# A hybrid decoder block: x handed over by feature as well and normed where it lands, weights handed over in blocks of 128 columns

## The chip, the cores and the metric

The kernel runs on one core of one Trainium2 chip. The metric is the device time of one execution in microseconds (us). A core has five engines that work beside one another: TensorE (PE: matmuls, with its weight loads PEld), VectorE (DVE), ScalarE (ACT), GpSimd (POOL) and SyncE (SP, which here only issues DMAs). Each engine takes its instructions in order. DMAs are issued from SP's and ACT's queues and move data between HBM and the on-chip memory SBUF; PE writes to PSUM, from where DVE and ACT read.

## What is computed

One decoder layer over x of 1024 tokens with 1024 features, float32. What the change touches is the beginning:

```python
def rms_norm(x, g):
    y = x * lax.rsqrt(jnp.mean(x * x, axis=-1, keepdims=True) + NORM_EPS)
    return y * g

u = rms_norm(h, mix_pre_g)                    # h is x here
z = jnp.einsum('bsd,de->bse', u, w_in)        # 1024 x 1024 by 1024 x 4096
p, q, k, v, gate_a, gate_b = (column ranges of z)
```

From q, k and v follows a differential attention of four heads, from p a pooling mixer; sigmoid gates merge both, an output projection, a residual with a norm, and a SwiGLU feed-forward with a hidden width of 2816 (w_ffn_gate, w_ffn_up, w_ffn_down) close the layer.

## The kernel before

Matmuls contract over the partitions, so u is needed by feature: 128 features on the partitions, tokens along the free dimension. Each float32 operand is split into a high part, rounded to the matmul's format (fp32r), and a low part, the rest; a product is three matmuls: high by high, high by low, low by high. `split` is an ACT copy (high) and a DVE subtract (low; `sub`, line 87).

The opening (lines 299 to 544) norms x and makes the first four of the 32 column blocks of z, which are q and k of heads 0 and 1 (f = 0 to 3), by plain matmuls. The rest of z is made by units (`unit`, `seven_steps`, line 271) that do two column blocks with seven block products in place of eight (Strassen's scheme). A unit needs the operands A11, A12, A21, A22 (the halves of u by token and by feature), their sums S1 to S4, and the like combinations B and T of two weight blocks; its products accumulate in PSUM banks X, Y and Z. Y takes its bank from the ring "mm", which the outputs of f = 2 and 3 also use; Z from "fil", which f = 0 and 1 use.

Inside the block `tc.manual_schedule` (line 463) the order of each of PE, ACT, DVE and POOL is the order in which the instructions are written. Outside it, and for SP, a planner with a cost model of its own sets the order. DMAs on ACT's queue stand in ACT's order.

In the opening, x comes in eight blocks of 128 tokens (tb = 0 to 7). For each: `stat` squares and sums it on ACT (`square`, line 363) and makes 1/rms (`rstd_of`, line 124: a DVE tensor_scalar, then a POOL pow); `normed` (line 371) multiplies the block by 1/rms, one number per partition, and by the gain g1, which was loaded onto all partitions, on DVE; `turn` (line 391) transposes it on PE in eight 128x128 steps into a PSUM pair; `take` (lines 405 to 421) copies it from there on ACT twice, as the high part of A and as a raw copy; `take_lo` makes the low part on DVE; `take_sums` (line 423), for the second half of the tokens, makes the sums on DVE. `feature(f, p)` is the product of block f with 256 tokens (p = 0 to 3): 24 matmuls (lines 357 for p = 0, 106 to 108 for the others). `store` (line 440) scales and splits its 512 columns (ACT and DVE), and `post` issues the store to `qkd` on ACT's queue. `first_raw`, `first_hi`, `first_lo` load and split the four weight blocks. `raw_weights` (line 211) loads 128 columns of a weight with 1024 rows: each of the 128 partitions gets eight runs of 512 bytes. `weights_steps` (line 216) makes the operands B and T of a unit. `constants` loads six small tensors on ACT's queue.

Of the kernel before, what the change touches and what calls it, by code (L numbers as in the profile page):

```python
# [39 lines left out]
def block_kernel(ctx, tc, x, w_in, pool_mix, pool_scale, w_branch_a, lam_q1, lam_k1, lam_q2,  # L40
# [4 lines left out]
    w_in, pool_mix, pool_scale, w_branch_a = w_in[0], pool_mix[0], pool_scale[0], w_branch_a[0]  # L45
# [3 lines left out]
        t[0] for t in (mix_pre_g, mix_post_g, ffn_pre_g, ffn_post_g))  # L49
    w_ffn_gate, w_ffn_up, w_ffn_down = w_ffn_gate[0], w_ffn_up[0], w_ffn_down[0]  # L50
# [262 lines left out]
    def w_cols(o, i):  # L313
        return w_in[:, o + i * P:o + (i + 1) * P]
# [6 lines left out]
    def qk_done(h, e, t, src, st=None, post=None):  # L321
        st = b4([P, 2, HALF], F32R, "qk_st") if st is None else st[e][:, :, half(t)]
        hi, lo = st[:, 0], st[:, 1]
        if e == 0:
            qs = 1.0 / (8.0 * 0.25 ** (h + 1))
            nc.scalar.mul(hi, src, qs)
            nc.vector.scalar_tensor_tensor(out=lo, in0=src, scalar=qs, in1=f32(hi), op0=ALU.mult, op1=ALU.subtract)
# [9 lines left out]
    plain, xts, xr = {}, [], []  # L337
# [14 lines left out]
    def common(h, e, t, o, c, by_pass):  # L352
        _, hi, lo = plain[h, e]
        if by_pass:
            for i, (w, a) in enumerate(((hi, 0), (hi, 1), (lo, 0))):
                for k in range(KD):
                    nc.tensor.matmul(o[:, c], w[:, k, :], U[f"A{t + 1}{k // 4 + 1}"][a][:, k % 4, c],
                                     start=i == 0 and k == 0, stop=i == 2 and k == KD - 1)
# [4 lines left out]
    def square(tb):
        ss = small(1, "ss")
        sumsq(xts[tb], ss)
        xr.append(ss)

    def rstd(tb):
        xr[tb] = rstd_of(xr[tb], 1, D)

    def normed(tb):
        nc.vector.scalar_tensor_tensor(out=xts[tb], in0=xts[tb], scalar=xr[tb], in1=g1, op0=ALU.mult, op1=ALU.mult)

    xts.append(load_x(0))
    xts.append(load_x(1))
    nc.sync.dma_start(g1, mix_pre_g.partition_broadcast(P))
    first_raw(0)
    xts.append(load_x(2))
    xts.append(load_x(3))
    first_raw(1)  # L380
    first_raw(2)
    xts.append(load_x(4))
    first_raw(3)

    turned = {}

    def stat(tb):
        square(tb)
        rstd(tb)

    def turn(tb):
        both = pair("x_t")
        for k in range(KD):
            nc.tensor.transpose(both[:, k // 4, k % 4 * P:(k % 4 + 1) * P], xts[tb][:, k * P:(k + 1) * P], ident)
        turned[tb] = [both[:, kq, :].rearrange("p (k t) -> p k t", k=4) for kq in range(2)]
        if tb + 5 < NB:
            xts.append(load_x(tb + 5))

    def token_cols(tb):
        return slice(tb % 4 * P, (tb % 4 + 1) * P)  # L400

    def raw_cols(tb, kq):
        return traws[(("A11", "A12"), ("S1", "S3"))[tb // 4][kq]][:, :, token_cols(tb)]

    def take_hi(tb):
        for kq in range(2):
            nc.scalar.copy(U[f"A{tb // 4 + 1}{kq + 1}"][0][:, :, token_cols(tb)], turned[tb][kq])
# [10 lines left out]
    def take_lo(tb):
        for kq in range(2):
            hi, lo = (a[:, :, token_cols(tb)] for a in U[f"A{tb // 4 + 1}{kq + 1}"])  # L420
            sub(lo, turned[tb][kq] if tb < 2 else raw_cols(tb, kq), hi)

    def take_sums(tb):
        s1, s2, s3, s4 = (traws[f"S{i + 1}"][:, :, token_cols(tb)] for i in range(4))
# [5 lines left out]
    outs, W = {}, {}  # L430
    wsteps = weights_steps(W, w_cols(o_q, 2), w_cols(o_k, 2))

    def feature(f, p):
        if p % 2 == 0:
            outs[f] = (fil if f < 2 else mm)("qk")
        common(*firsts[f], p // 2, outs[f], slice(p % 2 * 2 * P, (p % 2 + 1) * 2 * P), p == 0)

    posts = []

    def store(f, t):  # L440
        qk_done(*firsts[f], t, outs[f], post=posts)

    def post():
        posts.pop(0)()

    def sum_operand(*names):
        for n in names:
            U[n] = operand(n)
            split(U[n], traws[n])
# [12 lines left out]

    with tc.manual_schedule(engines={nc.tensor.engine, nc.scalar.engine, nc.vector.engine, nc.gpsimd.engine}):
        stat(0)
        stat(1)
        normed(0)
        turn(0)
        normed(1)
        turn(1)
        first_hi(0)  # L470
        take_hi(0)
        take_hi(1)
        first_lo(0)
        take_lo(0)
        take_lo(1)
        stat(2)
        normed(2)
        take_raw(0)
        feature(0, 0)
        first_hi(1)  # L480
        first_lo(1)
        take_raw(1)
        turn(2)
        stat(3)
        first_hi(2)
        normed(3)
        first_lo(2)
        feature(1, 0)
        take(2)
        stat(4)  # L490
        take_lo(2)
        turn(3)
        normed(4)
        first_hi(3)
        feature(2, 0)
        first_lo(3)
        take(3)
        stat(5)
        take_lo(3)
        turn(4)  # L500
        normed(5)
        take(4)
        stat(6)
        take_lo(4)
        take_sums(4)
        feature(3, 0)
        turn(5)
        take(5)
        normed(6)
        take_lo(5)  # L510
        stat(7)
        feature(0, 1)
        normed(7)
        take_sums(5)
        feature(1, 1)
        turn(6)
        store(0, 0)
        take(6)
        take_lo(6)
        take_sums(6)  # L520
        post()
        store(1, 0)
        next(wsteps)
        feature(2, 1)
        turn(7)
        take(7)
        constants()
        take_lo(7)
        post()
        store(2, 0)  # L530
        take_sums(7)
        feature(3, 1)
        post()
        store(3, 0)
        next(wsteps)
        post()
        sum_operand("S1")
        feature(0, 2)
        feature(1, 2)
        next(wsteps)  # L540
        feature(2, 2)
        sum_operand("S2")
# [8 lines left out]
        post()
        feature(1, 3)
        store(1, 1)
        sum_operand("S3")
        post()
# [93 lines left out]
    nc.scalar.mul(sgc, sgc, 1.0 - LAMBDA_INIT)  # L649
# [669 lines left out]
```

## Time and profile before

| what | us |
|---|---|
| median of 3 runs | 1265.39 (1264.96 to 1266.09) |
| the profiled execution | 1264.89 |
| its span, first to last instruction | 1263.0 |
| PE busy, DVE busy, ACT busy, POOL busy in the span | 1240.5, 822.2, 574.2, 226.6 |

The profile is one execution. Its page gives the busy time of each engine and the groups of instructions; the trace behind it can be asked for a timeline, for the waits of an engine (who it waited for; total, number, longest), and for windows of time. The granted clock of PE was 0.999 of the full one over the span. "128x512 f32" is a shape: partitions by elements.

### The profile page before, as it was taken

To read this page: it belongs to the slowest core of one execution; us is meant where nothing else is said; L and a number is where in the kernel's file an instruction comes from. 1 tells how busy PE (TensorE), PEld (TensorE's weight loads), DVE (VectorE), ACT (ScalarE), POOL (GpSimd) and SP (SyncE) were. 2 spreads that over 40 slices of the span, in tenths; PEclk is the share of its full clock that TensorE was granted. 3 is DMA by queue.
4 is the path that set the end of the run, shared out by engine and by line. 5 is a ranking of instruction groups with operands and counts; after the bars stand their busy time and mean duration, and the time that the engine had idled before them with its cause. 6 is when DMAs were issued, how large, how long until landed. Compare 5 with 4: busy or idle time off the path is not lost.

```text
span 1263.0 us, 15954 instructions
## 1 busy us (share of the span) xinstructions
PE 1240.5 (98%) x5952; PEld 1037.5 (82%) x5952; DVE 822.2 (65%) x1213; ACT 574.2 (45%) x1030; POOL 226.6 (18%) x237
## 2 busy tenths in 40 slices
PE   6999999999999999999999999999999999999997
PEld 6988778888888987888888888888888888888886
DVE  6895775445467776755697755656656537955666
ACT  7452344434567782444553333333333333554542
POOL 1000000000478861000102212112112011000221
PEclk9999999999999999999999999999999999999999
DMA  9263337234599213623315333233333368733235
GB/s 283 80 207 121 136 139 227 79 128 150 223 264 258 82 51 110 233 92 126 117 54 147 113 113 108 76 108 109 108 114 99 98 205 281 245 95 106 83 102 208
DMA packets 135566, 179.18 MB, mean 142 GB/s; under 512 B 7872, under 2 KB 90304, under 8 KB 133056
## 3 DMA queue, kind: packets, MB, share of 16 engines
q1 hardware_dynamic: 123552, 146.56, 37.2%
q10 hardware_dynamic: 11936, 31.60, 6.6%
q8 instruction: 47, 0.77, 0.3%
q14 instruction: 31, 0.25, 0.1%
HBM read 124.39 MB, written 53.74 MB: 141 GB/s over the span
## 4 chain that ended last, share of the span: by engine, by line
PE 87%; DVE 5%; ACT 3%; issue 2%; POOL 1%; DMA 0%; ACTq 0%; DVEq 0%; SPq 0%; POOLq 0%
PE Y L246 10%; PE Y L248 10%; PE Y L247 10%; PE X L246 5%; PE X L247 5%; PE X L248 5%; PE Yd L247 3%; PE Yd L248 3%; PE Yd L246 3%; PE o L812 3%; PE Z L248 2%; PE Z L247 2%; PE Z L246 2%; PE branch L248 2%; PE branch L247 2%
## 5 line engine op out<-in xcount | busy, mean ns | idle before, releaser
L164 DVE TENSOR_TENSOR p<-Z,p 128x512 f32<-128x512 f32 x35 | 24.2, 690 | 156.2 <-PE Z L248 154.5
L247 PE MATMUL Y<-A_lo,Wh 128*128 128x512 f32 x296 | 115.7, 391 | 0.3 <-DVE A_lo L87 0.3
L248 PE MATMUL Y<-A_hi,Wl 128*128 128x512 f32 x296 | 115.3, 389 | 0.1
L246 PE MATMUL Y<-A_hi,Wh 128*128 128x512 f32 x296 | 115.3, 390 | 0.0
L246 PE MATMUL Y<-S_hi,Wh 128*128 128x512 f32 x280 | 109.3, 390 | 0.0
L247 PE MATMUL Y<-S_lo,Wh 128*128 128x512 f32 x280 | 109.2, 390 | 0.0
L248 PE MATMUL Y<-S_hi,Wl 128*128 128x512 f32 x280 | 109.1, 389 | 0.0
L207 ACT CAST Wh<-wf_t 128x1024 fp32r<-128x1024 f32 x70 | 72.8, 1053 | 61.5 <-PE X L248 35.4
L87 DVE TENSOR_TENSOR Wl<-wf_t,Wh 128x1024 fp32r<-128x1024 f32 x70 | 86.9, 1247 | 13.9 <-PE Y L247 9.3
L87 DVE TENSOR_TENSOR w_op<-wd,w_op 128x512 fp32r<-128x512 f32 x77 | 56.3, 731 | 51.6 <-ACT w_op L168 51.4
L168 ACT CAST w_op<-wd 128x512 fp32r<-128x512 f32 x77 | 47.9, 622 | 71.4 <-PE Yd L248 31.2
L164 DVE TENSOR_TENSOR wf_t<-w_raw,wf_t 128x512 f32<-128x512 f32 x70 | 75.6, 1080 | 1.0
L247 PE MATMUL Yd<-w_op,s_op 128*128 128x512 f32 x176 | 68.7, 390 | 0.3 <-DVE w_op L87 0.2
L246 PE MATMUL Yd<-w_op,s_op 128*128 128x512 f32 x176 | 68.6, 390 | 0.0
L248 PE MATMUL Yd<-w_op,s_op 128*128 128x512 f32 x176 | 68.3, 389 | 0.0
L247 PEld LDWEIGHTS Y<-A_lo,Wh 128*128 128x128 f32 x296 | 55.6, 188 | 11.9 <-DVE A_lo L87 0.7
L248 PEld LDWEIGHTS Y<-A_hi,Wl 128*128 128x128 f32 x296 | 55.6, 188 | 11.9 <-DVE Wl L87 0.5
L246 PEld LDWEIGHTS Y<-A_hi,Wh 128*128 128x128 f32 x296 | 55.6, 188 | 11.6 <-ACT Wh L207 0.2
L168 ACT CAST s_op<-s_raw 128x512 fp32r<-128x512 f32 x77 | 47.5, 616 | 36.0 <-DMA s_raw<-fsd 23.3
L97 POOL TENSOR_TENSOR wb_lo<-wb_raw,wb_hi 128x1024 fp32r<-128x1024 f32 x4 | 10.5, 2632 | 291.8 <-DVE Wl L87 291.8
L246 PEld LDWEIGHTS Y<-S_hi,Wh 128*128 128x128 f32 x280 | 52.5, 188 | 12.1 <-ACT u L288 0.6
L248 PEld LDWEIGHTS Y<-S_hi,Wl 128*128 128x128 f32 x280 | 52.6, 188 | 10.9
(281 smaller groups left out, 3344.0 us busy)
## 6 DMA issues: line engine op xcount, KB each, us to landing
s_raw<-fsd SPq DMA_DIRECT2D x35, 512.0 KB, 3.8
w_raw<-in_w_in_dram SPq DMA_DIRECT2D x32, 512.0 KB, 4.2
w_raw<-in_w_ffn_gate_dram SPq DMA_DIRECT2D x22, 512.0 KB, 3.8
w_raw<-in_w_ffn_up_dram SPq DMA_DIRECT2D x22, 512.0 KB, 3.9
fsd<-fss SPq DMA_DIRECT2D x11, 1024.0 KB, 3.9
wd<-in_w_ffn_down_dram SPq DMA_DIRECT2D x44, 256.0 KB, 5.4
fsd<-F SPq DMA_DIRECT2D x33, 256.0 KB, 2.0
qkd<-qk_st ACTq DMA_DIRECT2D x16, 512.0 KB, 3.9
```

The costliest lines, as they stand in the source:

```text
L87: nc.vector.tensor_tensor(out=o, in0=a, in1=f32(hi), op=ALU.subtract)
L97: nc.gpsimd.tensor_tensor(out=lo, in0=raw, in1=f32(hi), op=ALU.subtract)
L164: nc.vector.tensor_tensor(out=o, in0=a, in1=b, op=op)
L168: nc.scalar.copy(hi, a)
L207: nc.scalar.copy(hi, a)
L246: nc.tensor.matmul(o, ah, bh, start=start, stop=False, skip_group_check=goes_on)
L247: nc.tensor.matmul(o, ah, bl, start=False, stop=False, skip_group_check=goes_on)
L248: nc.tensor.matmul(o, al, bh, start=False, stop=stop, skip_group_check=goes_on)
L812: nc.tensor.matmul(o, ats[b // 4][:, j, b % 4 * P:(b % 4 + 1) * P], V[:, b, :, :], start=b == 0 and j == 0, stop=b == qb and j == 1)
```

## The change

x is handed over a second time as `x_t`, by feature: four pieces of 256 tokens, each in two halves of 512 features (kq = 0, 1); on the chip a half is 128 partitions by 4 feature blocks by 256 tokens, and in memory each partition's 4 KB lie in one run. `w_in`, `w_ffn_gate` and `w_ffn_up` are handed over in blocks of 128 columns, in which the 4 KB of a partition also lie in one run. The gain comes as `g8`, 128 partitions by 8, one number for each feature.

x by token is still loaded and squared. 1/rms is now made for two token blocks at once (`rank`), copied along 128 columns on DVE, and turned by two PE transposes into a PSUM tile in which every partition holds 1/rms of the 256 tokens (`spread_rstd`). The piece is normed where it landed: for piece 0 one DVE instruction for each feature block multiplies by g8 and by the spread 1/rms (`normed_chunk`); for pieces 1 to 3 POOL multiplies by g8 (`scaled`, eight instructions a piece) and DVE by the spread 1/rms (`normed`, two a piece). High and low parts and sums are then made of 128x1024 each. The transposes of x and the raw copies are gone.

In the order: the four blocks' outputs are taken out of PSUM by two ACT instructions (`keep_raw`) and split later on DVE (`settle`), whose store to `qkd` goes to SP's queue; the loads of the constants go to SP too; the sums S1 to S4 are split in two halves each; the weights' steps of the first unit come later in the order; some arithmetic on constants that the planner placed moves to the end of the written order (`lambdas`).

```diff
     def raw_weights(src, tag):
         r = wp.tile([P, 2, 4, P], F32, tag=tag, bufs=2, name=name("w_raw"))
-        nc.sync.dma_start(r.rearrange("p h k n -> p (h k) n"), src.rearrange("(k p) n -> p k n", p=P))
+        nc.sync.dma_start(r.rearrange("p h k n -> p (h k n)"), src)
         return r
...
-    traws = {n: a8([P, 4, HALF], F32, n + "_raw") for n in ("A11", "A12", "S1", "S3")}
+    traws = {n: a8([P, 2, 4, 2 * P], F32, n + "_raw") for n in ("A11", "A12", "S1", "S3")}
     traws["S2"], traws["S4"] = traws["A11"], traws["A12"]
-    g1 = b4([P, D], F32, "g1")
+    g8 = cp.tile([P, KD], F32, name="g8")
+    nc.scalar.dma_start(g8, mix_pre_g)
...
     def w_cols(o, i):
-        return w_in[:, o + i * P:o + (i + 1) * P]
+        return w_in[o // P + i]
...
+    RAWS = (("A11", "A12"), ("S1", "S3"))
+    def raw_piece(p, kq):
+        return traws[RAWS[p // 2][kq]][:, p % 2]
+    def fetch_t(p, kq):
+        nc.sync.dma_start(raw_piece(p, kq).rearrange("p k t -> p (k t)"), x_t[p, kq])
...
+    def feature_pass(f, p, i):
+        _, hi, lo = plain[firsts[f]]
+        if p % 2 == 0 and i == 0:
+            outs[f] = (fil if f < 2 else mm)("qk")
+        w, a = ((hi, 0), (lo, 0), (hi, 1))[i]
         for k in range(KD):
-            nc.tensor.transpose(both[:, k // 4, k % 4 * P:(k % 4 + 1) * P], xts[tb][:, k * P:(k + 1) * P], ident)
...
+            nc.tensor.matmul(outs[f][:, piece_cols(p)], w[:, k, :], operand_piece(p, k // 4)[a][:, k % 4, :],
+                             start=i == 0 and k == 0, stop=i == 2 and k == KD - 1)
+    def feature(f, p):
+        for i in range(3):
+            feature_pass(f, p, i)
...
+    def square(p):
+        ss = small(2, "ss")
+        for i in range(2):
+            sumsq(xts.pop(2 * p + i), ss[:, i:i + 1])
+        ranks[p] = ss
+    def rank(p):
+        ranks[p] = rstd_of(ranks[p], 2, D)
+    def spread_rstd(p):
+        r = ranks[p]
+        rep = sm.tile([P, 2, P], F32, tag="sg", bufs=2, name=name("rep"))
+        nc.vector.tensor_copy(rep, r.unsqueeze(2).to_broadcast([P, 2, P]))
+        o = pair("r")[:, 0, :2 * P]
+        for i in range(2):
+            nc.tensor.transpose(o[:, i * P:(i + 1) * P], rep[:, i, :], ident)
+        spread[p] = o
+    def normed_chunk(p, k):
+        v = raw_piece(p, k // 4)[:, k % 4, :]
+        nc.vector.scalar_tensor_tensor(out=v, in0=v, scalar=g8[:, k:k + 1], in1=spread[p], op0=ALU.mult, op1=ALU.mult)
+    def scaled(p, kq):
+        for k in range(4):
+            v = raw_piece(p, kq)[:, k, :]
+            nc.gpsimd.tensor_scalar(v, v, g8[:, 4 * kq + k:4 * kq + k + 1], None, op0=ALU.mult)
+    def normed(p):
         for kq in range(2):
-            nc.scalar.copy(U[f"A{tb // 4 + 1}{kq + 1}"][0][:, :, token_cols(tb)], turned[tb][kq])
...
+            v = raw_piece(p, kq)
+            tt(v, v, spread[p].unsqueeze(1).to_broadcast([P, 4, 2 * P]), ALU.mult)
+    def piece_hi(p, kq):
+        nc.scalar.copy(operand_piece(p, kq)[0], raw_piece(p, kq))
+    def piece_lo(p, kq):
+        hi, lo = operand_piece(p, kq)
+        sub(lo, raw_piece(p, kq), hi)
+    def chunks(kq):
+        for k in range(4):
+            normed_chunk(0, 4 * kq + k)
+        piece_hi(0, kq)
...
+    def keep_raw(f, t):
+        h, e = firsts[f]
+        st = kept[f, t] = b4([P, 2, HALF], F32R, "qk_st")
+        qs = 1.0 / (8.0 * 0.25 ** (h + 1)) if e == 0 else 1.0
+        nc.scalar.mul(st[:, 0], outs[f], qs)
+        nc.scalar.mul(f32(st[:, 1]), outs[f], qs)
+    def settle(f, t):
+        h, e = firsts[f]
+        st = kept.pop((f, t))
+        sub(st[:, 1], f32(st[:, 1]), st[:, 0])
+        nc.sync.dma_start(qkd[h][e][:, :, half(t)], f32(st))
...
     def constants():
-        nc.scalar.dma_start(psc, pool_scale.rearrange("(g p) -> p g", p=P))
...
+        nc.sync.dma_start(psc, pool_scale.rearrange("(g p) -> p g", p=P))
```

SP's loads are written in the order x 0, x 1, x_t (0,0), weight 0, x_t (0,1), weights 1 and 2, x 2, x 3, weight 3, x_t (1,0), (1,1), x 4, x 5, x_t (2,0), (2,1), x 6, x 7, x_t (3,0), (3,1). The written order of the four other engines now reads (calls side by side, in order):

```python
square(0); rank(0); spread_rstd(0); first_hi(0); chunks(0); chunks(1)
feature_pass(0, 0, 0); first_lo(0); first_hi(1); piece_lo(0, 0); piece_lo(0, 1)
feature_pass(1, 0, 0); feature_pass(0, 0, 1); first_hi(2); first_lo(1); feature_pass(0, 0, 2); square(1)
feature_pass(1, 0, 1); first_lo(2); rank(1); scaled(1, 0); scaled(1, 1)
feature_pass(1, 0, 2); first_hi(3); first_lo(3); feature_pass(2, 0, 0); feature_pass(2, 0, 1)
spread_rstd(1); feature_pass(2, 0, 2); normed(1); piece_hi(1, 0); piece_hi(1, 1); square(2)
feature(3, 0); piece_lo(1, 0); piece_lo(1, 1); scaled(2, 0); rank(2); scaled(2, 1)
feature(0, 1); feature_pass(1, 1, 0); spread_rstd(2); feature_pass(1, 1, 1); feature_pass(1, 1, 2)
normed(2); square(3); piece_hi(2, 0); piece_hi(2, 1); scaled(3, 0); rank(3); scaled(3, 1)
piece_lo(2, 0); piece_lo(2, 1); keep_raw(0, 0); keep_raw(1, 0); feature(2, 1); feature_pass(3, 1, 0)
spread_rstd(3); normed(3); feature_pass(3, 1, 1); feature_pass(3, 1, 2); keep_raw(2, 0)
piece_hi(3, 0); piece_hi(3, 1); piece_lo(3, 0); piece_lo(3, 1); settle(0, 0); settle(1, 0)
feature(0, 2); keep_raw(3, 0); piece_sums(0); feature(1, 2); next(wsteps); settle(2, 0); settle(3, 0)
piece_sums(1); sum_operand("S1"); feature(2, 2); next(wsteps); feature(3, 2); sum_operand("S2"); next(wsteps)
feature(0, 3); keep_raw(0, 1); feature(1, 3); keep_raw(1, 1); sum_operand("S3"); constants(); next(wsteps)
feature(2, 3); keep_raw(2, 1); feature(3, 3); keep_raw(3, 1); next(wsteps, None); sum_operand("S4"); lambdas()
```

After it, outside the written order, come the four last calls of settle.

More of the change, by code (lines that the diff above doesn't have):

```diff
@@ L363, in square @@
[L363 to L392, printed above, removed]
-        for k in range(KD):
[L394 to L400, printed above, removed]
@@ L418, in take_lo, with piece_cols, operand_piece @@
[L418 to L424, printed above, removed]
+    def piece_cols(p):
+        return slice(p % 2 * 2 * P, (p % 2 + 1) * 2 * P)
+    def operand_piece(p, kq):
+        return [a[:, :, piece_cols(p)] for a in U[f"A{p // 2 + 1}{kq + 1}"]]
@@ new lines, in block_kernel @@
+    ranks, spread = {}, {}
+    def square(p):
[13 more added lines that the diff above has]
+        spread[p] = o
@@ L428, in take_sums @@
         tt(s4, s4, s2, ALU.subtract)
[L430 to L449, printed above, removed]
@@ L463, in block_kernel @@
[L463 to L542, printed above, removed]
@@ new lines, in sum_operand @@
+    def sum_operand(n):
+        U[n] = operand(n)
+        for j in range(2):
+            split([t[:, :, j * 2 * P:(j + 1) * 2 * P] for t in U[n]], traws[n][:, j])
+    kept = {}
+    def keep_raw(f, t):
[9 more added lines that the diff above has]
+        nc.sync.dma_start(qkd[h][e][:, :, half(t)], f32(st))
@@ new lines, in block_kernel @@
+    fetch_x(0)
+    fetch_x(1)
+    fetch_t(0, 0)
+    first_raw(0)
+    fetch_t(0, 1)
+    first_raw(1)
+    first_raw(2)
+    fetch_x(2)
+    fetch_x(3)
+    first_raw(3)
+    fetch_t(1, 0)
+    fetch_t(1, 1)
+    fetch_x(4)
+    fetch_x(5)
+    fetch_t(2, 0)
+    fetch_t(2, 1)
+    fetch_x(6)
+    fetch_x(7)
+    fetch_t(3, 0)
+    fetch_t(3, 1)
+    wsteps = weights_steps(W, w_cols(o_q, 2), w_cols(o_k, 2))
+    with tc.manual_schedule(engines={nc.tensor.engine, nc.scalar.engine, nc.vector.engine, nc.gpsimd.engine}):
+        square(0)
+        rank(0)
+        spread_rstd(0)
+        first_hi(0)
+        chunks(0)
+        chunks(1)
+        feature_pass(0, 0, 0)
+        first_lo(0)
+        first_hi(1)
+        piece_lo(0, 0)
+        piece_lo(0, 1)
+        feature_pass(1, 0, 0)
+        feature_pass(0, 0, 1)
+        first_hi(2)
+        first_lo(1)
+        feature_pass(0, 0, 2)
+        square(1)
+        feature_pass(1, 0, 1)
+        first_lo(2)
+        rank(1)
+        scaled(1, 0)
+        scaled(1, 1)
+        feature_pass(1, 0, 2)
+        first_hi(3)
+        first_lo(3)
+        feature_pass(2, 0, 0)
+        feature_pass(2, 0, 1)
+        spread_rstd(1)
+        feature_pass(2, 0, 2)
+        normed(1)
+        piece_hi(1, 0)
+        piece_hi(1, 1)
+        square(2)
+        feature(3, 0)
+        piece_lo(1, 0)
+        piece_lo(1, 1)
+        scaled(2, 0)
+        rank(2)
+        scaled(2, 1)
+        feature(0, 1)
+        feature_pass(1, 1, 0)
+        spread_rstd(2)
+        feature_pass(1, 1, 1)
+        feature_pass(1, 1, 2)
+        normed(2)
+        square(3)
+        piece_hi(2, 0)
+        piece_hi(2, 1)
+        scaled(3, 0)
+        rank(3)
+        scaled(3, 1)
+        piece_lo(2, 0)
+        piece_lo(2, 1)
+        keep_raw(0, 0)
+        keep_raw(1, 0)
+        feature(2, 1)
+        feature_pass(3, 1, 0)
+        spread_rstd(3)
+        normed(3)
+        feature_pass(3, 1, 1)
+        feature_pass(3, 1, 2)
+        keep_raw(2, 0)
+        piece_hi(3, 0)
+        piece_hi(3, 1)
+        piece_lo(3, 0)
+        piece_lo(3, 1)
+        settle(0, 0)
+        settle(1, 0)
+        feature(0, 2)
+        keep_raw(3, 0)
+        piece_sums(0)
+        feature(1, 2)
+        next(wsteps)
+        settle(2, 0)
+        settle(3, 0)
+        piece_sums(1)
+        sum_operand("S1")
+        feature(2, 2)
+        next(wsteps)
@@ L547, in block_kernel @@
         feature(3, 2)
+        sum_operand("S2")
+        next(wsteps)
         feature(0, 3)
-        store(0, 1)
-        next(wsteps)
[L551 to L555, printed above, removed]
+        keep_raw(0, 1)
+        feature(1, 3)
+        keep_raw(1, 1)
+        sum_operand("S3")
+        constants()
+        next(wsteps)
         feature(2, 3)
-        store(2, 1)
+        keep_raw(2, 1)
+        feature(3, 3)
+        keep_raw(3, 1)
         next(wsteps, None)
-        post()
@@ L560, in block_kernel @@
-        feature(3, 3)
-        store(3, 1)
         sum_operand("S4")
-        post()
+        lambdas()
+    for f in range(4):
+        settle(f, 1)
     later = []
```

79 lines of the change are left out of this document (35 added, 44 removed).

## The prediction, made before the change was timed

> **What bounds the kernel now.** The page comes first: its span line, the busy time of each engine and the row of PE in 40 slices.
>
> ```profile
> span 1263.0 us, 15954 instructions
> PE 1240.5 (98%) x5952; PEld 1037.5 (82%) x5952; DVE 822.2 (65%) x1213; ACT 574.2 (45%) x1030; POOL 226.6 (18%) x237
> PE   6999999999999999999999999999999999999997
> ```
>
> TensorE (PE) is busy in every slice but the first and the last. The PE waits come next: the first three rows are of the window 0 to 67.83 us, the others of the rest.
>
> ```profile
> PE x_t L394 <- DVE xt L372: 9.6, 3, 8.8
> PE qk L106 <- DVE qk_st L327: 1.1, 1, 1.1
> PE qk L357 <- ACT A_hi L407: 0.7, 1, 0.7
> ...
> PE oT L846 <- DVE O L833: 1.1, 2, 0.8
> PE y L106 <- ACT yh L168: 1.0, 2, 0.7
> PE h_t L1114 <- DVE og L1108: 0.7, 1, 0.7
> ```
>
> No row after the opening names a DMA, and these sum to a few microseconds. So the later weight loads are covered by PE work, and their new layout is worth nothing to the end; what the change does must come from the opening. That is what the timeline of PE shows, up to the first product of the first Strassen unit (X at 67.83):
>
> ```profile
> 8.75 3.53 PE L394 MATMUL x_t<-ident,xt 128*128 128x128 f32 x16 [8.75 <-DVE xt L372]
> 12.96 1.22 PE L357 MATMUL qk<-A_hi,w_hi 128*128 128x256 f32 x8 [0.68 <-ACT A_hi L407]
> 14.18 1.34 PE L357 MATMUL qk<-A_lo,w_hi 128*128 128x256 f32 x8
> ...
> 16.87 1.07 PE L394 MATMUL x_t<-ident,xt 128*128 128x128 f32 x8 [0.41 <-DVE xt L372]
> 17.69 1.20 PE L357 MATMUL qk<-A_hi,w_hi 128*128 128x256 f32 x8
> 18.73 1.12 PE L357 MATMUL qk<-A_lo,w_hi 128*128 128x256 f32 x8
> 19.69 1.12 PE L357 MATMUL qk<-A_hi,w_lo 128*128 128x256 f32 x8
> 67.83 0.40 PE L246 MATMUL X<-S_hi,Wh 128*128 128x512 f32 x1
> ```
>
> ```profile
> core 0: us, PE busy (x) PEld busy (x) DVE busy (x) ACT busy (x) POOL busy (x), PEclk, DMA share, GB/s
> 0.00:12.96 12.96, 3.53 (x17) 3.28 (x17) 5.01 (x9) 6.31 (x10) 1.80 (x8) 1.00 0.84 277
> 12.96:67.83 54.87, 52.81 (x433) 51.61 (x433) 47.98 (x75) 35.62 (x59) 4.82 (x10) 1.00 0.50 158
> 67.83:86.88 19.05, 19.05 (x85) 15.29 (x84) 16.02 (x19) 12.11 (x16) 0.00 (x0) 1.00 0.59 180
> ```
>
> The opening is 12.96 us before the first product and 54.87 us of products. A pass of 8 takes 0.96 us (18.73 to 19.69), 0.12 each, so the 384 take 46.1. The six later turns take about 0.82 each (16.87 to 17.69), 4.9 together. The remaining 3.9 us are slow first passes (12.96 to 14.18 is 1.22) and waits. VectorE (DVE) is busy for 48 of these 55 us, so it is the next bound. From 67.83 on PE is full, and what X gains the end gains.
>
> **The start.** x(0) and x(1) still come first, so the two squares stay where they are. Rows of ACT, DVE and POOL, then two windows of DMA rate:
>
> ```profile
> 4.58 1.06 ACT L132 ACTIVATE junk<-xt 128x1024 bf16<-128x1024 f32 x1 [2.58 <-DMA xt<-in_x_dram]
> 5.93 1.06 ACT L132 ACTIVATE junk<-xt 128x1024 bf16<-128x1024 f32 x1 [0.20 <-DMA xt<-in_x_dram]
> 7.11 0.15 DVE L127 TENSOR_SCALAR ms<-ss 128x1 f32<-128x1 f32 x1 [1.19 <-ACT junk L132]
> 7.34 0.56 POOL L128 TENSOR_TENSOR rstd<-ms,mhalf 128x1 f32<-128x1 f32 x1 [0.78 <-DVE ms L127]
> ```
>
> ```profile
> 3.00:5.00 2.00, 0.00 (x0) 0.00 (x0) 0.00 (x0) 0.42 (x1) 0.00 (x0) 1.00 1.04 420
> 12.00:15.00 3.00, 2.33 (x17) 1.81 (x16) 2.60 (x6) 2.68 (x6) 0.14 (x1) 1.00 1.17 299
> ```
>
> Rows of x alone came at 420 GB/s (3 to 5 us), loads mixed with weights at 299. In the changed kernel x, x by feature and weights all lie in 4 KB runs, so I take 1.27 us for each 512 KB (524 KB / 420 = 1.25); the other end is 1.75 (524 / 299). From 4.5 us on: x(1) 5.8, the two first feature pieces 7.0 and 9.6, weights 8.3, 10.9, 12.1 and 15.9, x(2) 13.4, x(3) 14.7, second feature pieces 17.2 and 18.5, last one 28.6. The 32-byte rows of g8 on ACT's queue land beside these.
>
> Durations for the new operations, and two pairs in which DVE and GpSimd (POOL) meet:
>
> ```profile
> L87 DVE TENSOR_TENSOR ml<-m,mh 128x256 fp32r<-128x256 f32 x32 | 12.5, 420 | 23.9 <-ACT mh L962 23.9
> L372 DVE SCALAR_TENSOR_TENSOR xt<-xt,rstd,g 128x1024 f32<-128x1024 f32 x8 | 10.2, 1282 | 2.2 <-POOL rstd L128 2.1
> L87 DVE TENSOR_TENSOR w_lo<-w_raw,w_hi 128x1024 fp32r<-128x1024 f32 x4 | 4.9, 1221 | 0.9 <-ACT w_hi L346 0.9
> L164 DVE TENSOR_TENSOR S_raw<-S_raw,S_raw 128x512 f32<-128x512 f32 x4 | 2.7, 683 | 0.0
> L781 POOL TENSOR_SCALAR E<-E,rec,cf 128x256 f32<-128x256 f32 x4 | 2.2, 558 | 0.4
> L829 POOL TENSOR_TENSOR rstd<-ms,mhalf 128x4 f32<-128x4 f32 x2 | 2.0, 1019 | 5.9 <-DVE ms L828 5.8
> ```
>
> ```profile
> 383.27 2.13 POOL L782 TENSOR_TENSOR E<-E,E 128x896 f32<-128x896 f32 x1
> 383.76 1.66 DVE L827 SCALAR_TENSOR_TENSOR ms<-esum 128x8 f32<-128x8 f32 x1
> ```
>
> ```profile
> 22.41 1.29 DVE L87 TENSOR_TENSOR A_lo<-A_raw,A_hi 128x512 fp32r<-128x512 f32 x2
> 22.57 0.93 POOL L128 TENSOR_TENSOR rstd<-ms,mhalf 128x1 f32<-128x1 f32 x1 [3.38 <-DVE ms L127]
> ```
>
> After the squares (7.1): one tensor_scalar and a pow over two columns, which lies between 0.56 (128x1) and 1.02 (128x4); I take 0.65, so 8.2. The spreading copy of 128x256 is not in the trace: at least the 0.15 of a one-column row, at most the 0.42 of a 128x256 subtract; 0.35. Two cold transposes at 0.22 (16 in 3.53) give 9.5. Each chunk of 128x256 costs 0.42, with 0.34 from start to start (the rows of DVE overlap by about 0.08); four end at 11.0, eight at 12.3. ScalarE's (ACT) cast of 128x1024 (at most the 1.06 of a square of that shape) ends at 12.1. **The first product starts at 12.2**, against 12.96, and the second half of its pass waits until 13.6 for the other cast. So the start itself gains 0.8 at most.
>
> **PE after that.** 384 products, 46.1. Six transposes remain, three spreads of 0.22: 0.7. The cold passes: before lost 0.26 in the first (1.22 against 0.96); here no run of 16 transposes stands ahead, so I take 1.2 over the first three, with 0 and 2.4 as ends. Waits, found by laying each engine's instructions in the written order at these durations: 0.6 for the other half of the first piece, 0.2 for w_hi(1), 0.1 for piece 1's second cast, 1.1 and 0.3 at spreads 2 and 3, whose copy stands behind rank on POOL. Sum: 12.2 + 46.1 + 0.7 + 1.2 + 2.3 = **62.5 us for the end of the products**, against 67.83.
>
> What is late next is piece 1: its columns land at 18.5, POOL scales eight chunks (at 0.60 with issue, 4.8 for a piece), DVE multiplies twice 1.2 and ACT casts; all is there at 26.6, and PE wants it at 26.5. Pieces 2 and 3 are wanted 11.5 us apart (96 products at 0.12), and none of the engines needs more than 6 for one, so they are hidden.
>
> **DVE.** After 12.3 it has, up to the low part of T1 and T3 that X needs: 12 subtracts of 128x1024 for weights and pieces at 1.14 (1.22 long, 1.14 apart) 13.7, six multiplies at 1.2 7.2, three copies 1.1, ranks 0.2, four settles at 0.6 2.4, eight sums of 128x1024 at 1.14 9.1, S1 and S2 4.6, two weight subtracts 2.3 and two differences 1.2: 41.8, so 54.1 without a wait. Waits add 8.0 (2.1 before the spread of piece 1, 3.1 around that of piece 2, the rest shorter). That is 62.1. **X can start at 62.6**, behind the products, and DVE has 0.4 us to spare, where before the same subtract ended 8.6 us ahead of X:
>
> ```profile
> 58.03 1.22 DVE L87 TENSOR_TENSOR Wl<-wf_t,Wh 128x1024 fp32r<-128x1024 f32 x1
> ```
>
> **Edits at nothing.** ACT loses 16 copies of 128x512 and gains eight for keep_raw; it waits for DVE, not the other way. The six constant loads and the eight stores go past ACT to SP, where behind them stand only weight loads for a unit that starts 19 us later; on ACT they held the queue ahead of the 1.1 us wait for qk_st, and that goes. The constants' arithmetic stands at the end of DVE's order; the four last settles (2.4) follow, with unit 2's weights behind them, needed near 82. Without that slack the 2.4 would count. Against the profiled run, X moves from 67.83 to 62.6: 5.2 us. That run took 1264.89 (span 1263.0 and 1.9 around it), and the median shown is 0.5 above it. **Forecast: 1259.7 us.**
>
> **The lock.** DVE's 8-column operation took 1.66 and ended with POOL's (385.42 against 385.40), and POOL's pow took 0.93 instead of 0.56 beside a subtract. One waits for the other. I have counted this where the 24 scalings meet a subtract or the copy: 0.9 us in the 62.5, which would be 61.6 if they never waited. The multiplies by spread are counted as free of it; if they too held POOL off, pieces 1 and 2 would each come 1.2 later (one multiply beside the scalings of each), and X would start near 64. The Trainium skill (SBUF — State Buffer, "SBUF: two separate sides") has it that the port pair these two engines share is locked for a whole instruction, by a GpSimd operation or by a DVE one with two SBUF inputs. By that rule a multiply whose second operand lies in PSUM takes no lock, so the sum would stay at 62.5, and every subtract that meets a scaling is paid in full; both quoted pairs agree with it, and no row of this trace has a multiply of this form beside POOL.
>
> **Rivals.**
> 1. **Slower: the scalings on POOL become the bound.** For: nothing in the opening put elementwise work on POOL, and the 0.93 row shows a wait of 0.37 on a 0.56 operation. At 0.93 for each, piece 1 is ready 2.6 us later (8 x 0.33), piece 3's spread, behind 16 more, costs 2.7, and X, which must then wait for T1 and T3, starts near 69.3 to 70, 1.5 to 2.2 after before's 67.83: 1266.4 to 1267.1, and each further 0.1 adds 2. It decides from about 0.78 on each; below that the kernel still gains. Against: the 558 ns row holds in the attention, where DVE works beside POOL, and the scaling there has two scalars and two operations against one here. Chance 0.12.
> 2. **The first unit takes Y first.** Y's bank is freed by keep_raw(2,1), which on ACT stands behind the cast of T2 and T4, and that behind DVE: 65.3. PE then waits 2.8 us: 1262.5, with a late DVE 1264. Against: before starts with X and Z, which use other banks. Chance 0.12.
> 3. **The pieces come at the mixed rate.** At 1.6 to 1.75 us for 512 KB, products end at 64.6 to 66.3: 1261.8 to 1263.5. For: 299 GB/s at 12 to 15 us. Against: those loads had rows of 512 bytes. Chance 0.12.
> 4. **More is gained.** Scalings at 0.5, no cold passes, Z ahead of X: 61 to 60: 1257.5. Chance 0.14.
> That x is not transposed any more is certain from the code; the forecast itself has 0.50.
>
> **How the numbers follow.** The forecast's own range is 1258.5 to 1261.5. For 8 in 10 I leave out the slower end of the first rival and half of the best case: 1257.3 to 1265. A measurement of this kernel can tell 0.2%, 2.5 us. Faster by more than that is below 1262.9: forecast 0.50, the best case 0.14, half of the second rival and of the third, 0.12: 0.76, taken down to 0.70 for waits I have not seen, which go to the two other cases. Slower (above 1267.9): half of the first rival, 0.06, and 0.03 of those waits. The rest, 0.21, is no change.
>
> **What would show it.** The x_t transposes are gone; eight transposes write r; the first qk product starts at 12.2 and X (or Z) near 62.6; POOL shows 24 tensor_scalar of 128x256 near 0.56; the PE waits in the opening stay under 0.7 each but at spread 2. Wrong: scalings at 0.8 or more, a PE wait over 2 us for A_hi of the second piece or for Wl at X, or a first Y that waits for qk_st.

## The result, and the profile after

| what | before | after |
|---|---|---|
| median, us (12 runs each) | 1265.32 (1264.81 to 1266.09) | 1268.48 (1267.74 to 1270.18) |
| the profiled execution, us | 1264.89 | 1268.47 |
| its span, us | 1263.0 | 1266.7 |

The ratio is 1.0026 (95% interval 1.0018 to 1.0034): the change makes the kernel slower by 3.2 us. The forecast was 1259.7 with a range up to 1265.0. The first two lines are of the page after, the third is the POOL row of before:

```profile
PE 1237.8 (98%) x5896; PEld 1034.7 (82%) x5896; DVE 821.3 (65%) x1207; ACT 571.2 (45%) x1018; POOL 250.1 (20%) x257
POOL 4400000000468861000102212112112011000221
POOL 1000000000478861000102212112112011000221
```

PE has 56 instructions less than before (64 transposes out, 8 in) and POOL 20 more (24 scalings in, four pows out); the first two slices of the row are the opening. Where the time went shows in windows cut at two marks: the first X product and the first Yd product (the last of the three large parts, w_ffn_down). First before, then after; the columns are those of the window rows in the prediction.

```profile
0.00:67.83 67.83, 56.35 (x449) 54.89 (x449) 52.99 (x83) 41.92 (x68) 6.62 (x18) 1.00 0.57 181
67.83:1045.59 977.76, 973.82 (x4583) 809.66 (x4581) 619.07 (x898) 434.39 (x776) 192.62 (x196) 1.00 0.42 136
1045.59:1263.00 217.41, 210.30 (x925) 173.00 (x923) 150.12 (x233) 97.91 (x188) 27.34 (x23) 1.00 0.49 158
```

```profile
0.00:69.68 69.68, 53.14 (x393) 52.06 (x393) 45.78 (x56) 34.54 (x48) 29.94 (x38) 0.95 0.56 214
69.68:1048.27 978.59, 974.12 (x4583) 809.67 (x4582) 625.31 (x919) 438.70 (x784) 192.75 (x196) 1.00 0.41 136
1048.27:1266.70 218.43, 210.57 (x925) 173.00 (x923) 150.22 (x233) 97.94 (x188) 27.36 (x23) 0.99 0.50 158
```

Of the 3.7 us by which the spans differ, 1.85 lie ahead of X, 0.83 in the long middle and 1.02 in the tail. In the opening PE is busy 3.2 us less than before, as meant, and still X starts later, not 5.2 us earlier. The waits of PE up to X, after:

```profile
PE r L398 <- DVE rep L395: 10.9, 2, 8.3
PE qk L374 <- ACT A_hi L416: 5.6, 3, 2.8
```

8.3 and 2.8 are the start, before the first product. The others are 2.61 for the fourth spread, 2.42 for the second piece and 0.35. What the first two of these wait for is on POOL, whose timeline after has no gap from 18.11 to 46.6 us:

```profile
18.11 0.71 POOL L128 TENSOR_TENSOR rstd<-ms,mhalf 128x2 f32<-128x2 f32 x1 [10.17 <-DVE ms L127]
18.81 8.12 POOL L408 TENSOR_SCALAR A_raw<-A_raw,g 128x256 f32<-128x256 f32 x8
26.92 5.22 POOL L408 TENSOR_SCALAR S_raw<-S_raw,g 128x256 f32<-128x256 f32 x4
32.11 0.73 POOL L128 TENSOR_TENSOR rstd<-ms,mhalf 128x2 f32<-128x2 f32 x1
32.83 9.01 POOL L408 TENSOR_SCALAR S_raw<-S_raw,g 128x256 f32<-128x256 f32 x8
41.80 0.72 POOL L128 TENSOR_TENSOR rstd<-ms,mhalf 128x2 f32<-128x2 f32 x1
42.53 3.75 POOL L408 TENSOR_SCALAR S_raw<-S_raw,g 128x256 f32<-128x256 f32 x4
46.24 0.41 POOL L473 IOTA cnt<- 128x16 f32 x4
```

The 24 scalings fill 26.1 us, 1.09 each, where the forecast had 0.60. DVE, whose multiplies need them, runs without a gap from the last of these multiplies up to X:

```profile
26.97 1.22 DVE L164 TENSOR_TENSOR A_raw<-A_raw,r 128x1024 f32<-128x1024 f32 x1 [2.39 <-POOL A_raw L408]
46.31 1.22 DVE L164 TENSOR_TENSOR S_raw<-S_raw,r 128x1024 f32<-128x1024 f32 x1 [1.64 <-POOL S_raw L408]
68.67 1.22 DVE L87 TENSOR_TENSOR Wl<-wf_t,Wh 128x1024 fp32r<-128x1024 f32 x1
```

The chain is this: the last scaling ends at 46.28, the last multiply starts at 46.31, and 22 us of DVE work behind it end at 69.89 with the low part that X needs. PE comes to X with its own products at the same time and does not wait; the second of these rows is the first product that reads the low part:

```profile
69.68 0.40 PE L246 MATMUL X<-S_hi,Wh 128*128 128x512 f32 x1
70.14 0.39 PE L248 MATMUL X<-S_hi,Wl 128*128 128x512 f32 x1
```

POOL waits for nothing after 18.11 and DVE for nothing after 46.31, so by this profile a faster PE would have brought that product forward by 0.25 us at most.

### The profile page after: what moved, and what is told of

Same layout as the page of the kernel before. It is cut to its first block, busy times and chain, and to the rows that moved or that the text cites. A ratio compares the mean times of both kernels' runs of the same rounds, so it can differ in the third digit from the quotient of the medians.

```text
span 1266.7 us, 15858 instructions
## 1 busy us (share of the span) xinstructions
PE 1237.8 (98%) x5896; PEld 1034.7 (82%) x5896; DVE 821.3 (65%) x1207; ACT 571.2 (45%) x1018; POOL 250.1 (20%) x257
## 4 chain that ended last, share of the span: by engine, by line
PE 47%; DVE 1%; issue 1%; POOL 1%; DMA 0%; ACT 0%; DVEq 0%; POOLq 0%; ACTq 0%
PE Y L247 6%; PE Y L248 6%; PE Y L246 6%; PE X L246 3%; PE X L247 3%; PE X L248 3%; PE Yd L247 3%; PE Yd L248 3%; PE Yd L246 3%; PE Z L247 2%; PE Z L248 2%; PE Z L246 2%; PE Xd L248 2%; PE Xd L246 2%; PE Xd L247 2%
## 5 line engine op out<-in xcount | busy, mean ns | idle before, releaser
L87 DVE TENSOR_TENSOR Wl<-wf_t,Wh 128x1024 fp32r<-128x1024 f32 x70 | 86.8, 1248 | 15.3 <-PE Y L247 9.8
```

The costliest lines, as they stand in the source:

```text
L87: nc.vector.tensor_tensor(out=o, in0=a, in1=f32(hi), op=ALU.subtract)
```

## The experiments

All times are medians in us. The kernel before was timed beside them on the same chip: 1265.26 beside the first four, then 1265.41 (the unread input, the filled waits, the early ranks), 1265.44 (the two kernels after that) and 1265.27 (the tail's edit alone, in both kernels).

**What a scaling costs.** Three kernels ask for it. The first gives the scaling a second scalar from memory (a column of ones) and a second multiply:

```diff
-            nc.gpsimd.tensor_scalar(v, v, g8[:, ...], None, op0=ALU.mult)
+            nc.gpsimd.tensor_scalar(v, v, g8[:, ...], pone, op0=ALU.mult, op1=ALU.mult)
```

> The changed kernel with POOL's 24 scalings in the form that the attention uses: two scalars and two operations (the gain's column, then a column of ones), same result. Theory A (the form costs: one scalar and one operation took 0.92 us alone, two scalars took 0.56): the scalings are near 0.56 where DVE leaves them alone, X starts at 62.5 to 64 instead of 69.7, and the time is 1261 to 1263. Theory B (POOL is slow here for where the data lies or what runs beside it, not for the form): they stay near 0.92 and the time stays at 1268.5. Theory C (the scalings are not what delays the pieces; DMA or the ranks are): they get shorter and X still starts after 68.

Measured: 1261.31 (1260.87 to 1261.83, 6 runs), ratio 0.9970 (0.9958 to 0.9982). X starts at 62.80 in place of 69.68, and POOL is through at 38.90 in place of 46.24. The larger group of its POOL, with 0.69 us for each:

```profile
L410 POOL TENSOR_SCALAR S_raw<-S_raw,g,pone 128x256 f32<-128x256 f32 x16 | 10.9, 691 | 0.0
```

One added multiply by one turns the loss into a gain: this one term decided the sign.

The second takes POOL out: pieces 1 to 3 are normed like piece 0, by eight DVE instructions each.

```diff
-        for kq in range(2):
-            v = raw_piece(p, kq)
-            tt(v, v, spread[p].unsqueeze(1).to_broadcast([P, 4, 2 * P]), ALU.mult)
+        for k in range(KD):
+            normed_chunk(p, k)
```

> The changed kernel without POOL's scalings: pieces 1 to 3 are normed as piece 0 is, by eight DVE instructions of 128x256 that take the gain and the spread 1/rms at once. DVE gets 8 x 0.34 in place of 2 x 1.2 a piece, 0.3 us more, and POOL keeps only the ranks. Theory A: PE's waits for A_hi of the second piece and for the spreads of pieces 2 and 3 shrink below 1 us each, X starts at 61.5 to 63.5, time 1260.5 to 1263. Theory C: X stays after 68 and the time near 1268.

Measured: 1262.12 (1260.68 to 1264.22, 11 runs), ratio 0.9975 (0.9967 to 0.9984), X at 62.45. Eight chunks take DVE 3.22 us a piece against 2.35 for the two multiplies; DVE had the room. So POOL's price was the loss, and POOL isn't needed for the gain.

The third puts three forms side by side, one for each of pieces 1 to 3; in pieces 2 and 3 it leaves the gain out.

```diff
+            if p == 1:
+                nc.gpsimd.tensor_scalar(v, v, g8[:, ...], pone, op0=ALU.mult, op1=ALU.mult)
+            elif p == 2:
+                nc.gpsimd.tensor_scalar(v, v, 1.0, None, op0=ALU.mult)
+            else:
+                nc.gpsimd.tensor_scalar(v, v, 1.0, 1.0, op0=ALU.mult, op1=ALU.mult)
```

> Forms of the scaling in one kernel: piece 1 two scalars from memory and two operations, piece 2 one constant and one operation, piece 3 two constants and two operations; in pieces 2 and 3 the gain is left out (a factor of 1). The shortest durations of each piece are read. Theory A: 0.56 with two operations (pieces 1 and 3), 0.92 with one (piece 2). If a scalar read from memory is what costs: 0.92 in piece 1, less in 2 and 3. Theory B: all three near 0.92.

Measured: 1261.08 (one run). The view by tile gives shortest, median and longest duration in ns; the first two rows are of the changed kernel:

```profile
L408 POOL TENSOR_SCALAR S_raw<-S_raw,g x16: 916/923/2560, 26.9 to 45.4; 128x256 f32<-128x256 f32 x16
L408 POOL TENSOR_SCALAR A_raw<-A_raw,g x8: 917/921/1798, 18.8 to 26.0; 128x256 f32<-128x256 f32 x8
```

```profile
L411 POOL TENSOR_SCALAR A_raw<-A_raw,g,pone x8: 554/556/1432, 18.8 to 23.5; 128x256 f32<-128x256 f32 x8
L413 POOL TENSOR_SCALAR S_raw<-S_raw x8: 844/854/1471, 24.0 to 32.1; 128x256 f32<-128x256 f32 x8
L415 POOL TENSOR_SCALAR S_raw<-S_raw x8: 403/412/828, 32.9 to 37.7; 128x256 f32<-128x256 f32 x8
```

With one operation the instruction takes 0.85 to 0.92, with two 0.41 to 0.56, on the same shape. Whether the scalar is a constant or lies in memory moves it by 0.07 to 0.14; the count of operations by 0.36 to 0.44. With constants two operations took 0.41, less than the 0.56 expected. It is the form, not the data.

**The weights alone.** The kernel before with the blocks of 128 columns and nothing else:

```diff
-        return w_in[:, o + i * P:o + (i + 1) * P]
+        return w_in[o // P + i]
```

> The kernel before with only the weights handed over in blocks of 128 columns (rows of 4 KB); x as before. If the later weight loads are hidden, as forecast: the opening changes little (the first weight lands about 1 us sooner, but ACT and the transposes set the first product), X within 0.7 us of 67.83 and the time within 1 us of 1265.3. If the layout is what costs 1 to 2 us in the rest of the kernel: 1266.3 to 1267.3, with a wait for s_raw in the last 30 us.

Measured: 1265.56 (11 runs), ratio 1.0003 (0.9994 to 1.0012): no change. X starts at 68.09, 0.3 later than before, and no wait of PE names a load.

**PE's clock.** In the changed kernel the passes of eight behind the two long waits take 1.2 to 1.7 us in place of 0.96. Transposes that nobody reads fill the waits here:

```diff
+            if (f, p, i, k) == (0, 1, 0, 4):
+                filler(34, spare[1])
...
+        filler(36, spare[2])
         spread_rstd(3)
```

> The changed kernel with products that nobody reads in PE's two long waits of the opening: 34 transposes of the identity (0.07 us each in a row) after the first four products of f = 0 on the second piece, 36 ahead of the fourth spread. Theory C (the granted clock falls because PE stood still): passes of eight after these places take 0.96 us from start to start in place of 1.18 to 1.71, the granted clock between 30 and 35 us and between 45 and 50 us is 1.00 in place of 0.66 and 0.76, and the products behind run about 1.3 us earlier; X stays within 0.4 us of 69.7, since DVE holds it, and the span stays near 1266.7. Theory D (the clock falls for what the other engines do, or for the load after a wait): passes of 1.2 to 1.7 us and a clock of 0.66 to 0.76 stay.

Windows of the changed kernel, then of this one (the third column from the right is the granted clock):

```profile
32.00:33.00 1.00, 1.00 (x7) 1.00 (x7) 0.13 (x1) 0.97 (x3) 1.00 (x3) 0.50 0.99 393
30.00:35.00 5.00, 5.00 (x32) 5.00 (x31) 1.31 (x4) 3.77 (x8) 5.00 (x6) 0.66 0.74 284
45.00:50.00 5.00, 5.00 (x35) 5.00 (x34) 3.69 (x4) 2.83 (x4) 1.65 (x6) 0.76 0.01 3
```

```profile
30.00:35.00 5.00, 5.00 (x46) 5.00 (x45) 1.28 (x3) 3.82 (x8) 4.78 (x6) 1.00 0.74 287
45.00:50.00 5.00, 5.00 (x45) 5.00 (x44) 4.24 (x4) 2.94 (x4) 1.36 (x6) 1.00 0.00 0
```

The clock stays at 1.00, with about the same work on POOL and ACT beside, and the passes behind the fillers start 0.94 to 0.97 us apart (32.54, 33.48, 34.45, 35.41): with the waits filled there is no fall, so the fall came of PE's standing still. The fillers took 0.115 us each, not 0.07 as reckoned, and ran 2.3 to 2.7 us past the old waits, so X (70.47) is later here and says nothing on what the clock cost the end; by the profile of the changed kernel that was the 0.25 us above at most. It took 1268.46 (one run).

**The tail.** Where does the last 1.0 us come from? In the changed kernel ACT waits 1.2 us for the last load of s_raw; before, nobody does. SP's issues in the tail (and ACT's cast) of the changed kernel, then SP's of before:

```profile
1238.23 0.33 SPq L1251 DMA_DIRECT2D hr<-h1d  x1
1241.78 0.33 SPq L1207 DMA_DIRECT2D s_raw<-fsd  x1
1246.87 0.62 ACT L168 CAST s_op<-s_raw 128x512 fp32r<-128x512 f32 x1 [1.20 <-DMA s_raw<-fsd]
```

```profile
1234.31 0.33 SPq L1222 DMA_DIRECT2D hr<-h1d  x1
1239.10 0.33 SPq L1178 DMA_DIRECT2D s_raw<-fsd  x1
```

A load of 512 KB (hr) is issued ahead of it: 4.79 us ahead in the kernel before, 3.55 in the changed one. The load of s_raw itself isn't issued later: in both kernels its issue stands 193.51 us behind the first Yd. But it lands 5.1 us after its issue in place of 3.4. Is it the place of the data in memory, or the other load? First x by feature as an unread input of the kernel before:

```diff
+        nc.scalar.dma_start(xt8, x_t[0, 0][:, :8])
```

> The kernel before, with x by feature as a further input that lies in memory but of which only 4 KB are read (32 bytes for each partition, on ACT's queue beside the constants). It asks where the last 1.0 us of the loss comes from: in the kernels that hand x over twice, the last load of s_raw lands 5.1 to 6.0 us after its issue and ACT waits for it 1.2 to 1.4 us; in the kernel before and with blocks alone it lands after 2.8 to 4.0 and nobody waits. Theory P (place in memory): 4 MB more in front of the scratch tensors shift what the tail stores and loads, so the tail is slow here too: last load over 5 us, from the first Yd product to the end 218.4 us, span 1264.0. Theory T (timing: the changed opening shifts the phase of queues and planner): the tail stays as before: 217.4 us, no wait of ACT for s_raw, span 1263.0.

Measured: 1265.43 (one run); from the first Yd (1046.21) to the end (1263.5) 217.3, no wait of ACT for s_raw. So one more input of x's size in memory doesn't do it. The kernel with filled waits agrees: it has the whole change, its two issues are 4.78 apart (1237.93 and 1242.71), and its tail takes 217.5 (1049.22 to 1266.7). Then the order, in the changed kernel and in the one before; the edit gives hr other buffers, and with that its loads are issued behind the last of s_raw:

```diff
-        hr = wp.tile([P, D], F32, tag=("whi", "wlo")[tb % 2], bufs=2, name=name("hr"))
+        hr = b4([P, D], F32, "hr") if tb >= 4 else wp.tile(...)
```

> The changed kernel with the edit in the tail alone (the residual rows of token blocks 4 to 7 in other buffers, so that the last load of s_raw is issued ahead of the first of them). If the tail's share of the changed kernel's loss is that collision, it is 1.0 to 1.2 us faster than the changed kernel without it (1268.48): 1267.4 us, from the first Yd product to the end 217.3 us in place of 218.4, no wait of ACT for s_raw, and what is left against the kernel before is the opening and the first unit, 1.9 to 2.5 us. If the collision is of no account, the time stays at 1268.5.

> The kernel before with the same edit in the tail alone. Its last load of s_raw lands 3.4 us after issue and nobody waits for it, so by the collision theory the edit is worth nothing here: 1265.4 us, within 0.3, from the first Yd product to the end 217.4 us as before. If the edit is worth 1 us here too, the kernel before paid for the collision as well, and the tail is no part of the loss.

Measured: the changed kernel 1267.98 (1267.22 to 1268.66, 11 runs), ratio 1.0022 (1.0013 to 1.0031); the kernel before 1265.20 (11 runs), ratio 1.0000 (0.9991 to 1.0009). In the first one's profile the tail is 217.44 (1048.46 to 1265.9), as expected, and ACT's wait for s_raw 0.3. The median gained 0.5 and not 1.0 to 1.2, with ranges that overlap (1267.74 to 1270.18 without the edit); X was 0.34 later in this profile (70.02), which is part of the rest. The kernel before gains nothing.

**A better order.** With cheap scalings the rank of the fourth piece still stands behind POOL's work, and PE waits 1.11 us for it. First attempt, from the two-scalar kernel:

```diff
         spread_rstd(1)
+        square(2)
+        rank(2)
...
         piece_hi(2, 1)
-        scaled(3, 0)
         rank(3)
+        scaled(3, 0)
```

> Two-scalar scalings, and the squares and ranks of pieces 2 and 3 earlier: the square of piece 2 right behind the last weight cast, its rank ahead of the scaling of piece 2 on POOL and ahead of normed(1) on DVE; the square of piece 3 behind the casts of piece 1, its rank ahead of the scaling of piece 3. Two-scalar scalings alone gave 1261.31 us with X at 62.80, PE waiting 1.11 us for the fourth spread and DVE standing 3.3 us between 28 and 38 us. If the rest of the opening is the rank that stands behind POOL's scalings, the 1.11 us wait goes, X starts at 61.3 to 62.0, and the time is 1260.2 us (1259.7 to 1260.8). If DVE's own work holds X, X stays at 62.4 to 62.8 and the time at 1261.3.

Measured: 1262.51 (1261.57 to 1264.70, 11 runs), ratio 0.9979 (0.9970 to 0.9988): a miss, 1.2 slower than the two-scalar kernel. PE's wait is gone and X starts at 62.15, but on POOL the fourth rank now waits for DVE, and all of piece 3 stands behind it:

```profile
33.99 1.61 POOL L130 TENSOR_TENSOR rstd<-ms,mhalf 128x2 f32<-128x2 f32 x1 [2.86 <-DVE ms L129]
35.61 4.86 POOL L410 TENSOR_SCALAR S_raw<-S_raw,g,pone 128x256 f32<-128x256 f32 x8
```

DVE then stands 2.9 us for these, and X's third product 1.3 us for the weights' low part, so that product starts at 64.13 where the two-scalar kernel has 63.26. The profiled execution, at 1264.56, is 2 us above the median, and that lies elsewhere: its tail takes 220.59. There PE stands 1.15 us for ACT, and 1.5 us after its return the granted clock falls to 0.50 for about 3.4 us:

```profile
1242.51 0.50 PE L248 MATMUL Yd<-w_op,s_op 128*128 128x512 f32 x1 [1.15 <-ACT w_op L170]
1245.00:1246.00 1.00, 1.00 (x4) 0.80 (x3) 0.61 (x2) 0.00 (x0) 0.31 (x1) 0.50 0.97 287
```

How many of the other executions had this, no profile shows. The second attempt moves that rank ahead of DVE's multiplies:

```diff
         spread_rstd(2)
+        rank(3)
...
-        rank(3)
         scaled(3, 0)
```

> As the run with early ranks, but the fourth rank stands ahead of normed(2) on DVE and behind the scaling of piece 2 on POOL, so that neither it nor the scaling of piece 3 waits for DVE. In the run with early ranks POOL stood 2.86 us at that rank (33.99) and DVE then 2.9 us for piece 3, and X had to wait 1.3 us for the weights' low part. If POOL's order was the cause, piece 3 is multiplied from about 36.8 us on in place of 38.4 and 40.5, X starts at 61.7 to 62.3 with no wait for Wl, and the time is 1260.5 us (1259.8 to 1261.3), tail as in the two-scalar run. If DVE's work alone holds X, its last low part ends no sooner than 62.4 and the time is 1261.3 or more.

Measured: 1260.54 (1259.93 to 1261.43, 5 runs), ratio 0.9961 (0.9949 to 0.9974), X at 61.19, earlier than expected, and 0.2 of wait for Wl. Last, with the order of the tail as well:

> The last but one kernel with one more edit in the tail: the residual rows of token blocks 4 to 7 are loaded into other buffers, so that SP issues the last load of s_raw (256 KB) ahead of the first of them (512 KB) and not behind it. Theory Q (the last load of s_raw is late because a 512 KB load issued 3.2 to 3.8 us ahead of it is still on its way): it lands under 4 us after issue, ACT does not wait for it, from the first Yd product to the end is 217.3 us in place of 218.6, and the time is 1.0 to 1.3 us below the run without this edit: 1259.3. Theory R (stores or the memory itself slow it, whatever is ahead in the queue): it still lands over 5 us after issue, the wait of 1.2 to 1.7 us stays, and so does the time.

Measured: 1259.54 (1259.14 to 1260.18, 5 runs), ratio 0.9954 (0.9940 to 0.9967), the fastest of all. The window of its tail:

```profile
1040.29:1257.70 217.41, 210.31 (x925) 173.00 (x923) 149.88 (x233) 97.72 (x188) 27.36 (x23) 0.99 0.50 159
```

The tail is 217.41 as in the kernel before, and 218.56 without the edit (1040.14 to 1258.7): that is its 1.0 us. In the run without the edit ACT has no wait for s_raw; its lost time stands a few casts earlier, where two stores take it 2.17 us to issue (from 1234.31), and with the edit 1.00 (from 1234.46). So which row carries the loss differs. Shown is that the loss goes when hr's loads follow the last of s_raw; that it comes of two loads sharing the queue's time is a reading of this, since the edit changes order and buffers together.

## Why the prediction was wrong

**The step that failed** is "POOL scales eight chunks (at 0.60 with issue, 4.8 for a piece)". The scaling took 0.92 alone and 1.09 on the mean. The price came from the 558 ns row of the attention, the right shape with another form: two scalars and two operations. The first rival held just that against itself ("the scaling there has two scalars and two operations against one here"), as if fewer operations could not cost more. On this engine they did. The two-scalar kernel, whose scaling is that of the row, puts X at 62.80, where the forecast had 62.6.

**The first rival is what happened.** It gave 0.93 each and X at 69.3 to 70; measured are 0.92 and 69.68. It had a chance of 0.12, and its path is the one seen: PE waits of 2.42 and 2.61 where it priced 2.6 and 2.7, and then DVE's low part for X. But that the figures agree so closely is luck in part. It took its 0.93 from a pow that met a subtract, a GpSimd instruction held up by DVE, and the scaling takes its 0.92 undisturbed. The lock came on top of that, 1.09 on the mean, for which the rival's own rule (2 us for each further 0.1) gives an X about 3 us later than was measured. Two of the prediction's own signs of being wrong came: scalings over 0.8, and a PE wait over 2 us for A_hi of the second piece.

DVE's waits between the first product and X, which the forecast laid at 8.0, sum to 15.3 after:

```profile
DVE A_raw L164 <- POOL A_raw L408: 5.9, 2, 3.5
DVE rep L395 <- POOL rstd L128: 3.5, 2, 2.3
DVE S_raw L164 <- POOL S_raw L408: 2.4, 2, 1.6
DVE S_raw L164 <- PE r L398: 2.1, 2, 1.5
DVE ms L127 <- ACT junk L132: 1.0, 1, 1.0
DVE w_lo L87 <- ACT w_hi L354: 0.4, 1, 0.4
```

11.8 of these are POOL's.

**A second step failed in size:** "what X gains the end gains". After X the changed kernel loses 1.85 more, which is why the rival's 1266.4 to 1267.1 was too low as well; the two-scalar kernel loses 1.6 of its 5.0 (middle 978.21 and tail 218.59 against 977.76 and 217.41). The tail's 1.0 goes when its loads are put in another order. In the middle, 0.68 is a wait of the first unit's Y for ACT, which before doesn't have:

```profile
78.71 0.50 PE L246 MATMUL Y<-S_hi,Wh 128*128 128x512 f32 x1 [0.68 <-ACT p L282]
```

The two-scalar kernel has the same wait, at 71.82. The trace shows where it comes from: before, PE does three products of Z between the first Y and the second (75.34 to 76.17) while ACT copies Y out of PSUM (75.53 to 76.12); after, the second Y follows the first directly and stands until that copy is done (78.07 to 78.66). No run put the order back.

**Right:** the first product (12.2 forecast, 11.85 measured); pow over two columns (0.65, 0.71); the spreading copy (0.35, 0.29); eight chunks done at 12.3 (12.28); the loads (420 GB/s forecast, 408 to 417 over 5 to 20 us, so the third rival falls); no first Y that waits for qk_st, so the second falls; the weights' layout at nothing. PE's wait for qk_st is gone, as costed.

**Right only in sum:** the end of the products. In the two-scalar kernel the first 24 took 5.88 us against 2.88 for 24 later ones:

```profile
11.80 1.22 PE L376 MATMUL qk<-A_hi,w_hi 128*128 128x256 f32 x4 [2.83 <-ACT A_hi L418]
13.37 3.02 PE L376 MATMUL qk<-A_hi,w_hi 128*128 128x256 f32 x12 [0.35 <-ACT A_hi L418]
16.20 1.64 PE L376 MATMUL qk<-A_hi,w_lo 128*128 128x256 f32 x8
17.68 1.11 PE L376 MATMUL qk<-A_lo,w_hi 128*128 128x256 f32 x8
```

Less the wait of 0.35, that is 2.65 us lost in slow first passes, where I took 1.2 with 2.4 as the end. Waits of 1.46 in place of 2.3 and a start 0.4 earlier made up for most of it.

**The lock** was told rightly. Two pairs of the changed kernel, POOL's scalings first and what DVE did beside them:

```profile
33.86 2.73 POOL L408 TENSOR_SCALAR S_raw<-S_raw,g 128x256 f32<-128x256 f32 x3
34.68 1.22 DVE L164 TENSOR_TENSOR S_raw<-S_raw,r 128x1024 f32<-128x1024 f32 x1 [1.52 <-PE r L398]
37.47 3.46 POOL L408 TENSOR_SCALAR S_raw<-S_raw,g 128x256 f32<-128x256 f32 x2
37.88 2.35 DVE L87 TENSOR_TENSOR A_lo<-S_raw,A_hi 128x1024 fp32r<-128x1024 f32 x2
```

Beside a multiply whose second operand lies in PSUM the scalings take 0.91 each, as alone; beside subtracts 1.73. This agrees with the Trainium skill (SBUF — State Buffer, "SBUF: two separate sides"), which names DVE instructions with two SBUF inputs among those that take the shared port pair for a whole instruction. The forecast put it at 0.9 us of X; on POOL it is 26.1 us less 24 times 0.92 (22.1), 4.0, and what of that reached X no run shows. Of the 11.7 by which POOL is over the forecast's 14.4 (24 times 0.60) the form is 7.7.

**Open:** why the two loads of the tail are issued 3.2 to 3.9 us apart in most kernels with the change and 4.8 apart before, and by what the nearer one costs time; why no product of Z stands between the two Y any more, and what that costs the end; half of the tail edit's gain in the changed kernel.

## What to carry to other kernels

Take a duration from a row of the same engine, shape and form, down to the count of scalars and operations, and where only the shape agrees let the range reach as far as if the other form were dearer. Before work moves to an idle engine, sum it there in order of due time: POOL stood idle for most of the span and was the bound of 28 us of it. When an early gain is to reach the end, look at the last loads of the kernel too, since a shift can bring two of them closer together (3.55 us in place of 4.79 here).

## What the hardware showed that was not expected

- GpSimd's tensor_scalar of 128x256 float32 takes 0.85 to 0.92 us with one operation and 0.41 to 0.56 with two.
- PE's granted clock fell to 0.50 for about 3.4 us, starting 1 us after products came back from a wait of 2.42 us, and again after one of 2.61; each fall lengthened the next passes by 1.5 us. The Trainium skill (TensorE: Matmul & The Clock Gate, "What's actually happening") names an idle window of about 3.4 us for that; here shorter waits did it. The length of the wait alone doesn't decide: one of 1.11 us in the two-scalar kernel cost nothing (its clock was 1.00 from 30 to 45 us), and one of 1.15 in the tail of the run with early ranks was followed by the same fall.
- GpSimd's pow of 128x2 took 0.71 us alone and 1.61 to 1.67 beside DVE's subtracts.
